# A retention layer's output projection as seven products over sums of halves, with the heads in a new order and the gated outputs through DRAM

## The chip, the cores and the metric

The kernel runs on one core of one Trainium2 chip. The metric is device time in microseconds (us) of the whole kernel. Five engines work beside each other, each through a list of instructions of its own: PE (matrix products; PEld is its weight load), DVE (vector), ACT (scalar functions and copies), POOL (the third elementwise engine) and SP, which here only issues DMAs. An engine runs its list in order and halts at an instruction whose inputs or buffers are not ready.

## The reference

One sequence of 1024 positions, width 1024, passes a retention layer and then a stick-breaking attention layer. The change lies in the first layer and in what stands right behind it:

```python
u = rms_norm(h, ret_norm_pre[i])
q, k, v, g = jnp.split(u @ ret_w_in[i], [...], axis=-1)
q = rope(split_heads(q, 4), pos)
k = rope(split_heads(k, 4), pos) * 256 ** -0.5
o = retention_chunkwise(q, k, v)          # 4 heads, values 512 wide
o = (o - mu) * lax.rsqrt(var + EPS)       # per position and head
o = merge_heads(o) * jax.nn.silu(g)       # 1024 x 2048
y = o @ ret_w_out[i]                      # 2048 -> 1024
h = h + rms_norm(y, ret_norm_post[i])
kv = rms_norm(h, kv_norm) @ w_kv          # keys, values of the next layer
```

Retention is causal. In chunks of 128 positions, `o` is (q k^T * decay) v inside a chunk plus q times a state that is carried on.

## The kernel before, in words

**Arithmetic.** All is float32. For a product each operand is written as a rounded part (ACT copies it to fp32r) and the rest (DVE subtracts), which is `split`. `mm3` makes a product of three PE matmuls: high by high, high by low, low by high. Most are 128x512: 128 rows out, 512 columns.

**Tiling.** The sequence is taken in two halves of 512, t=0 and t=1. Activations lie transposed, 128 channels by 512 positions a tile. PSUM has eight banks of 512 floats in four tags with two buffers each: `pma`, `pmb` for projections, `pz`, `po` for the retention heads.

**Projections.** `Group` makes a projection of 1024 by 1024 with seven products in place of eight, over sums and differences of halves of the weights, of the input and of the output (numbered 1 to 7; each is 48 PE matmuls). Six groups (v0, g0, k, q, v1, g1) feed the retention layer, six more (K, Q, V0, G0, V1, G1) the attention layer.

**Retention heads.** `AHead(t, h)` is one head of one half. `scores()` makes q k^T, `mix()` the outputs `o` into the `po` banks (four tiles of 128 positions by 512), and for t=0 the state that t=1 of the same head needs, which goes to DRAM (`st`) and is read back. An output tile leaves its bank in one way: DVE takes its statistics (BATCH_NORM_STATS2, AGGREGATE), POOL makes the reciprocal root from them with three small operations, ACT writes the normed tile `sgn`. Only then is the `po` bank free. `gate()` multiplies with the gate, transposes on PE into `pz` and splits the result into `oT`.

**Output projection before.** `outproj` runs once for each (t, h): eight tiles of 128x512, 12 matmuls each, added into `y`, which lies in DRAM (`y_d`) and is read and written once a head. Its matmuls stand between the PE work of the next head: while U=(t, h) goes through `mix` and `gate` and the head behind it through `scores`, the projection of the head ahead of U fills PE. The order of heads is (0,0), (0,1), (0,2), (0,3), (1,0), ... The first head stands beside product 4 of group g1.

**Behind it.** `a_post(t)` norms `y` (sum of squares, a column of reciprocal roots on POOL, turned into a row of 512 by `diag` and a matmul), adds x and takes the sum of squares of the result; `c_stats(t)` and `c_prep` make from it the operands of the six attention groups. `a_post(0)` runs beside heads (1,1) and (1,2), half its sums on POOL; `a_post(1)` beside the products 2 of the second to sixth group.

**Order.** The program isn't issued as written. All operations are recorded (one helper, line 229, emits every one, so all lines read L229). `merge` puts the side work between the main matmuls, and `Plan` sets each engine's order by its own costs. What it decides is seen only in the lists of instructions.

Of the kernel before, what the change touches and what calls it, by code (L numbers as in the profile page):

```python
# [10 lines left out]
F32 = mybir.dt.float32  # L11
# [7 lines left out]
NH = 4  # L19
# [438 lines left out]
def trunk(ctx, tc, xT, wts, gains, trig, ident_in, cols, grow_in, out):  # L458
# [4 lines left out]
    BUFS = dict(b=28, f=25, big=2, whl=3, small=24, col=8, ma=2, mb=2, z=2, o=2)  # L463
    GROUP = dict(xh="b", v="b", A="b", AT="b", S="b", ko="b", sgn="b", sc0="b", sc1="b", sc2="f", sc3="f", wraw="f", f2="f",
                 sg="f", vo="f", tab="f", acc="f", qk="big", oT="big")
# [245 lines left out]
    def sumsq(acc, src, c, eng):  # L711
        if c == 0:
# [63 lines left out]
    h_d = [[DRAM(f"h{t}{c}", F32) for c in range(4)] for t in range(2)]  # L776
    av_d = [[[rec.tile(dr, [128, 512], F32, f"av{t}{h}{b}", dram=True) for b in range(4)] for h in range(NH)] for t in range(2)]
# [10 lines left out]
    def a_prep():  # L788
# [122 lines left out]
    class AHead:  # L911
        def __init__(self, t, h):
            self.t, self.h, self.base = t, h, 48 + 4 * h

        def fetch(self):
            x, h = [], self.h
            for n in range(4):
                raw = S("f2", [512])
                dma(raw[:], aqk_d[self.t][h][n][:])
                x.append(hl("ko"))  # L920
                split((x[n][:, 0, :], x[n][:, 1, :]), raw[:], None if h < 2 else -1.0)
            self.q, self.k = x[:2], x[2:]
            self.v = []
# [8 lines left out]
        def out(self, y_d, acc=None, hold=None):  # L932
            return outproj(self.base, lambda: self.oT, y_d, self.h == 0, acc, None, hold)
# [33 lines left out]
        def mix(self):  # L967
# [69 lines left out]
            os = [lambda ib=ib: o(ib) for ib in range(4)] + [normed]  # L1037
# [4 lines left out]
            return [state_in] + os  # L1042

        def gate(self):
            o = S("qk" if self.h == NH - 1 else "oT", [4, 2, 512], F32R)
            self.oT = [o[:, e] for e in range(4)]

            def step(ib):
                on = self.on[ib]
# [9 lines left out]
    def a_post(t, y_d, acc, hold=None):  # L1059
# [13 lines left out]
        def load(k):  # L1073
            y, raw = box[k] = (hold[k % 4][:, k // 4], S("tab", [512])) if t else (S("vo", [512]), S("vo", [512]))
            if not t:
                dma(y[:], y_d[k])
            dma(raw[:], xT[128 * k:128 * k + 128, HT * t:HT * t + HT])

        def add(k):
            c2, c = divmod(k, 2)  # L1080
            y, raw = box[k]
            V.scalar_tensor_tensor(y[:], y[:], gcol(G_POST, k), box["rows"][:], ALU.mult, ALU.mult)
            (V if t else G).tensor_tensor(y[:], y[:], raw[:], ALU.add)
            dma(h_d[t][c2][:, 512 * c:512 * c + 512], y[:])

        def square(k):
            y, raw = box[k]
            if k == 0:
                A_.activation(box["acc"][:], y[:], AF.Square)
            else:  # L1090
                A_.activation(raw[:], y[:], AF.Square)
                (V if t else G).tensor_tensor(box["acc"][:], box["acc"][:], raw[:], ALU.add)
# [4 lines left out]
        return [stat1, stat2, row] + in_turn(8, 3 if t else 0, load, add, square) + [stat3]  # L1097
# [34 lines left out]
    def h_rows(t, i, hold=None):  # L1132

        raw = S("S", [2, 512]) if hold is None else hold[i]
        for c in range(0 if hold else 2):
            dma(raw[:, c], h_d[t][i // 2 + 2 * c][:, 512 * (i % 2):512 * (i % 2) + 512])
        V.tensor_tensor(raw[:], raw[:], rowh[t][:].unsqueeze(1).broadcast_to([128, 2, 512]), ALU.mult)
        return raw

    def c_prep(hold):  # L1140
# [16 lines left out]
        def early(i, c):  # L1157
            if c:
                X.raw[i] = h_rows(0, i)
# [27 lines left out]
    class Group:  # L1187
        def __init__(self, base, kind, gain, X, banks, order, early=(), keep=True):
# [8 lines left out]
            self.starts.update({n: banks4 for n in early})  # L1197
            self.onto = {n: m for n, m in ((6, 1), (7, 1), (4, 1), (3, 5)) if n not in early}
# [94 lines left out]
        def chunks(self, *which):  # L1293
# [27 lines left out]
            def done(n, b, p):  # L1321
# [9 lines left out]
                if n == 6 or n in (1, 2) and not k(3 - n) or n == 5 and 7 not in early:  # L1331
# [19 lines left out]
                elif n == 7:  # L1351
                    self.put(0, 1, b, plus(k(5), p), -1)
# [41 lines left out]
    class CPair:  # L1394
# [57 lines left out]
        def mix(self, hh):  # L1452
# [44 lines left out]
            def gate():  # L1497
                for e in range(2):
# [3 lines left out]
                    if j == 0:  # L1502
                        self.o = S("oT", [4, 2, 512], F32R)
                    x = self.oT[j] = self.o[:, j]
# [99 lines left out]
    def run():  # L1604
# [12 lines left out]
        def make_groups(base, kinds, X, early, keep):  # L1617
            order = [tuple(n for n in ((1, 2, 6, 5, 7, 3, 4) if at < 5 else (2, 1, 6, 5, 3, 7, 4)) if n not in early[at]) for at in range(6)]
            return order, [Group(base + 8 * at, kind, gain, X, sets[::-1] if at % 2 and at < 5 else sets, order[at], early[at], keep[at])
# [5 lines left out]
        order, groups = make_groups(0, kinds, X, early, (True, False, True, True, False, True))  # L1625
        H = [[AHead(t, h) for h in range(NH)] for t in range(2)]
# [29 lines left out]
        units = [(t, h) for t in range(2) for h in range(NH)]  # L1656
        post, acc = [], []
        for k, (t, h) in enumerate(units):
            U = H[t][h]
            if k == 0:  # L1660
                continue
            t0, h0 = units[k - 1]
            if t0 == 1 and h0 == 0:
                post = a_post(0, y_d[0], acc)
            if h0 == 0:
                acc = []
            side = [(post[:5], 0, 0)] if (t, h) == (1, 1) else [(post[5:] + c_stats(0), 0, 0)] if (t, h) == (1, 2) else []
            if (t, h) == (1, 3):
                hold = []
                Y, load, plain, late = c_prep(hold)  # L1670
                side = [(load, 0, 0)]
            nxt = H[units[k + 1][0]][units[k + 1][1]] if k + 1 < 8 else None
            def sides(U=U, side=side, nxt=nxt):
                x = [(U.mix() + U.give + U.gate(), 0, 0)]
                if nxt:
                    x.append((nxt.scores(), 0, 0))
                return x + side
            go(H[t0][h0].out(y_d[t0], acc if h0 == 3 else None), sides)
        X = Y
# [3 lines left out]
        go(groups[0].chunks(2))  # L1683
        go(H[1][3].out(y_d[1], acc, hold))
        post = a_post(1, y_d[1], acc, hold)
        ahead_of = [(at, 2) for at in range(1, 6) if early[at]]
        steps = [[(post[:3], 1, 0)], [(plain + post[3:6], 0, 0)], [(post[6:9], 0, 0)], [(post[9:], 0, 0)], [(c_stats(1) + late[:2], 0, 0)]]
        for k, (at, n) in enumerate(ahead_of):
            go(groups[at].chunks(n), lambda k=k: steps[k] if k < len(steps) else [])
# [117 lines left out]
```

## Time and profile before

| | us |
|---|---|
| time, median of 3 runs (lowest, highest) | 1635.08 (1632.72, 1636.35) |
| profiled execution, first to last instruction (its span) | 1629.8 |
| PE busy | 1619.7 |
| DVE busy | 1247.6 |
| ACT busy | 818.6 |
| POOL busy | 246.9 |

The profiled execution's own time is its span and a few us around it: the median stands 5.3 us above the span. In the trace the first head's `mix` lies at about 464 to 491 us, the out projections of heads at about 491 to 800, five products 2 of the attention groups at about 800 to 855. A matmul record's length is longer than the distance to the next one, since matmuls overlap; PE's rate is read from the starts of two neighbouring rows.

### The profile page before, as it was taken

How to read it: one execution, taken by the hardware profiler on the slowest of the kernel's cores; microseconds unless marked ns; L12 is line 12 of the kernel's file. 1: busy time of each engine (PE TensorE's matmuls, PEld its weight loads, DVE VectorE, ACT ScalarE, POOL GpSimd, SP SyncE). 2: the span in 40 equal slices, each digit the busy share in tenths (PEclk: the TensorE clock that was granted, in tenths of full speed). 3: DMA queues.
4: the chain of work that ended last, by engine and by line, in shares of the span. 5: the costliest groups of instructions: out<-in, count | busy, mean ns of one | idle time of the engine just before them, and what ended most of it. 6: DMA issues, size and time to landing. Idle time of an engine off the chain costs nothing.

```text
span 1629.8 us, 23078 instructions
## 1 busy us (share of the span) xinstructions
PE 1619.7 (99%) x7634; PEld 1346.5 (83%) x7634; DVE 1247.6 (77%) x1952; ACT 818.6 (50%) x1502; POOL 246.9 (15%) x328
## 2 busy tenths in 40 slices
PE   9999999999999999999999999999999999999998
PEld 7888888888888888888888888888888888888886
DVE  7998679795686777767569966758658886879897
ACT  7634332322576545533467544545445655536544
POOL 0000024230022114441000000000002222212420
PEclk9999999999999999999999999999999999999999
DMA  8774636486477788788486879639787869777884
GB/s 287 247 249 162 226 122 215 155 299 224 155 251 247 265 291 277 263 303 298 163 291 209 311 261 335 245 134 312 260 329 255 294 230 308 265 275 275 287 283 155
DMA packets 201400, 407.99 MB, mean 250 GB/s; under 512 B 22592, under 2 KB 23232, under 8 KB 201280
## 3 DMA queue, kind: packets, MB, share of 16 engines
q1 hardware_dynamic: 201280, 406.51, 72.4%
q8 instruction: 60, 0.98, 0.2%
q14 instruction: 60, 0.49, 0.1%
HBM read 286.89 MB, written 119.54 MB: 249 GB/s over the span
## 4 chain that ended last, share of the span: by engine, by line
PE 77%; DVE 2%; issue 0%; ACT 0%; DVEq 0%
PE pma L229 21%; PE pmb L229 21%; PE po L229 19%; PE pz L229 16%; DVE f L229 1%; DVE whl L229 0%; DVE wraw L229 0%; ACT f L229 0%; ACT small L229 0%; DVEq L1802 0%; DVE col L229 0%; DVE A L229 0%; DVEq L229 0%
## 5 line engine op out<-in xcount | busy, mean ns | idle before, releaser
L229 ACT ACTIVATE whl<-wraw 128x512 fp32r<-128x512 f32 (+1 forms) x392 | 231.9, 626 | 299.6 <-PE pmb L229 95.9
L229 DVE TENSOR_TENSOR whl<-wraw,whl 128x512 fp32r<-128x512 f32 x392 | 275.3, 725 | 129.6 <-ACT whl L229 129.1
L229 PE MATMUL pmb<-oT,whl 128*128 128x512 f32 x552 | 144.7, 395 | 0.0
L229 PE MATMUL pma<-oT,whl 128*128 128x512 f32 x552 | 141.9, 396 | 0.0
L229 PEld LDWEIGHTS pma<-oT,whl 128*128 128x128 f32 x552 | 101.4, 188 | 20.3 <-ACT oT L229 0.2
L229 PE MATMUL pma<-whl,xh 128*128 128x512 f32 x456 | 117.5, 392 | 0.1
L229 PEld LDWEIGHTS pmb<-oT,whl 128*128 128x128 f32 x552 | 100.8, 188 | 19.1
L229 PE MATMUL pmb<-whl,xh 128*128 128x512 f32 x456 | 116.1, 389 | 0.0
L229 POOL TENSOR_SCALAR_AFFINE_SELECT f<-f 128x128 f32<-128x128 f32 x64 | 34.3, 551 | 492.3 <-DMA wraw<-in_wts_dram 384.0
L229 PE MATMUL pma<-xh,whl 128*128 128x512 f32 x408 | 105.0, 392 | 0.0
L229 PE MATMUL pmb<-xh,whl 128*128 128x512 f32 x408 | 103.9, 390 | 0.0
L229 PE MATMUL pz<-ko,ko 128*128 128x512 f32 (+3 forms) x480 | 101.6, 332 | 0.0
L229 PEld LDWEIGHTS pmb<-whl,xh 128*128 128x128 f32 x456 | 85.6, 188 | 18.0
L229 PEld LDWEIGHTS pma<-whl,xh 128*128 128x128 f32 x456 | 84.9, 188 | 18.3 <-DVE whl L229 0.5
L229 POOL TENSOR_TENSOR f<-f,f 128x512 f32<-128x512 f32 x32 | 51.6, 1624 | 253.1 <-DVE f L229 225.4
L229 PEld LDWEIGHTS pmb<-xh,whl 128*128 128x128 f32 x408 | 76.4, 188 | 15.8
L229 PEld LDWEIGHTS pma<-xh,whl 128*128 128x128 f32 x408 | 75.9, 188 | 16.1 <-issue 0.5
L229 PEld LDWEIGHTS pz<-ko,ko 128*128 128x128 f32 x480 | 77.0, 189 | 10.5 <-ACT A L229 1.2
L229 PE MATMUL pma<-whl,oT 128*128 128x512 f32 x312 | 82.0, 398 | 0.5 <-ACT oT L229 0.3
L229 PE MATMUL pmb<-whl,oT 128*128 128x512 f32 x312 | 81.2, 392 | 0.0
L229 DVE SCALAR_TENSOR_TENSOR wraw<-wraw,gn,wraw 128x512 f32<-128x512 f32 x96 | 69.8, 745 | 14.2 <-ACT wraw L229 8.9
L229 PE MATMUL pz<-xh,whl 128*128 128x512 f32 x312 | 79.2, 389 | 0.0
(207 smaller groups left out, 3334.8 us busy)
## 6 DMA issues: line engine op xcount, KB each, us to landing
wraw<-in_wts_dram SPq DMA_DIRECT2D x559, 256.0 KB, 5.1
v<-v SPq DMA_DIRECT2D x64, 512.0 KB, 6.1
y<-f SPq DMA_DIRECT2D x112, 256.0 KB, 2.7
f<-y SPq DMA_DIRECT2D x88, 256.0 KB, 4.9
ko<-kq SPq DMA_DIRECT2D x40, 512.0 KB, 5.7
kq<-v SPq DMA_DIRECT2D x32, 512.0 KB, 6.4
s<-f SPq DMA_DIRECT2D x40, 256.0 KB, 2.9
f<-s SPq DMA_DIRECT2D x40, 256.0 KB, 4.6
```

The source lines that it names most:

```text
L229: f(*[_real(a) for a in o.args], **{k: _real(v) for k, v in o.kw.items()})
```

## The change

- The output projection is one `AOut`: for all of `y` seven products (1, 5, 3, 6, 7, 4, 2 in this order) over sums of the two sequence halves, of the two halves of the 2048 inputs (heads 0, 1 and heads 2, 3) and of the two halves of the outputs. A product is 4 units x 2 x 4 banks x 3 = 96 matmuls.
- Its operands are made on DVE and ACT in tiles of 128x1024 (`op` from the gated outputs, `whl` from the weights), each sum or difference first, then the split. The gated outputs go to DRAM (`o_d`, 16 stores of 512 KB) and come back as often as products need them (36 loads of 512 KB); the weights take 36 loads of 512 KB in place of 64 of 256 KB.
- The heads are in the order (0,0), (1,0), (0,1), (1,1), (0,2), (0,3), (1,2), (1,3), called U0 to U7 here. U0 to U3 stand beside products 7, 4, 5, 3 of g1, U4 to U7 beside products 1, 5, 3, 6 of `AOut`. Product 7 has no side work, product 4 has the first part of `a_post(0)`, product 2 the rest of it with `c_stats(0)` and the first operands of the attention groups.
- `y` stays in SBUF (`hold`), so `y_d` isn't written or read; `a_post(0)` makes all its sums on DVE. The six products 2 of the attention groups follow, with `a_post(1)` beside the first four and `c_stats(1)` beside the fifth.
- Buffers: the pools `big` (2) and `whl` (3) become one pool `w` (7), of which `op`, `on`, `oT`, `qk` and `whl` take their tiles.

By the two programs' lists, PE has 7510 instructions (before 7606), which is 96 matmuls of 128x512 fewer; DVE 1944 (1954), ACT 1484 (1496), POOL 311 (333), and SP issues 1302 DMAs (1398): 176 of 256 KB fewer, 88 of 512 KB more.

The diff, cut:

```diff
-    BUFS = dict(b=28, f=25, big=2, whl=3, small=24, col=8, ma=2, mb=2, z=2, o=2)
+    BUFS = dict(b=28, f=25, w=7, small=24, col=8, ma=2, mb=2, z=2, o=2)
...
+    o_d = [[[DRAM(f"o{t}{h}{n}", F32) for n in range(2)] for h in range(NH)] for t in range(2)]
...
         def gate(self):
...
-                split((o[:, :, 0, il], o[:, :, 1, il]), pt[:].rearrange("p (e n) -> p e n", e=4))
+                A_.activation(o[:, :, il], pt[:].rearrange("p (e n) -> p e n", e=4), AF.Copy)
+                if ib == 3:
+                    for n in range(2):
+                        dma(o_d[self.t][self.h][n][:], o[:, 2 * n:2 * n + 2].rearrange("p a b -> p (a b)"))
...
+    class AOut:
...
+            self.units = [(n, i) for n in (1, 5, 3, 6, 7, 4, 2) for i in range(4)]
+            self.get = ahead(28, lambda at: (self.weights(*self.units[at]), self.operand(*self.units[at])))
...
+        def operand(self, n, i):
...
+            x = S("op", [2, 1024], F32R)
+            if n in (1, 2, 3):
+                a = load(*{1: (1, 0), 2: (1, 1), 3: (0, 1)}[n])
+            elif n in (5, 7):
+                a, b = (load(1, 0), load(0, 0)) if n == 5 else (load(0, 1), load(0, 0))
+                V.tensor_tensor(a[:], a[:], b[:], ALU.subtract)
...
+            split(self.pieces(x), a[:])
+            return x
...
+        def chunk(self, n, i, kk):
...
+            for b in range(4):
+                cl = slice(512 * kk + 128 * b, 512 * kk + 128 * b + 128)
+                mm3(banks[b][:], w[:, 0, cl], w[:, 1, cl], x[:, 0, sl], x[:, 1, sl], n != 3 and i + kk == 0, i == 3 and kk == 1, goes_on=n == 3)
...
-            (V if t else G).tensor_tensor(y[:], y[:], raw[:], ALU.add)
+            V.tensor_tensor(y[:], y[:], raw[:], ALU.add)
...
-        return [stat1, stat2, row] + in_turn(8, 3 if t else 0, load, add, square) + [stat3]
+        return [stat1, stat2, row] + in_turn(8, 3, load, add, square) + [stat3]
...
+        order, groups = make_groups(0, kinds, X, early, (True, False, True, True, False, True), (1, 2, 6, 7, 4, 5, 3))
+        order[4] = (1, 6, 4, 5, 3)
+        U = [AHead(t, h) for t, h in ((0, 0), (1, 0), (0, 1), (1, 1), (0, 2), (0, 3), (1, 2), (1, 3))]
...
-                go(group.chunks(*order[at][:-2]))
-                go(group.chunks(7), lambda: [(H[0][0].scores(), 0, 0)])
-                go(group.chunks(4), lambda U=H[0][0]: [(U.mix() + U.give + U.gate(), 0, 0), (H[0][1].scores(), 0, 0)])
+                go(group.chunks(1, 2))
+                go(group.chunks(6), lambda: [(U[0].scores(), 0, 0)])
+                for k, n in enumerate((7, 4, 5, 3)):
+                    go(group.chunks(n), unit(k))
...
-            go(H[t0][h0].out(y_d[t0], acc if h0 == 3 else None), sides)
-        X = Y
+        hold, acc = [[None] * 4 for _ in range(2)], [[], []]
+        Y = AOut(48, hold, acc)
+        for k, n in enumerate((1, 5, 3, 6)):
+            go(Y.chunks(n), unit(4 + k))
+        go(Y.chunks(7))
+        X, load, plain, late = c_prep(hold)
+        post0, post1 = a_post(0, acc[0], hold[0]), []
+        go(Y.chunks(4), lambda: [(post0[:9], 0, 0)])
+        go(Y.chunks(2), lambda: [(post0[9:] + c_stats(0) + load, 0, 0)])
```

**SP, the states of the first head.** Before, the list has the two stores of the state of (0,0) with weight loads, sums of `y` and the next head's inputs between and behind them; the loads `ko<-st_73`, `ko<-st_74` of (1,0) stand some hundred rows further on. After, the same place reads (`av` and `ag` are a head's values and gates in DRAM, `on` the gated outputs, `o` their place in DRAM):

```order
L229 DMA st_73<-ko_4427 128x1024 [waits DMAHW3_49,DVE_49]
L229 DMA sg_4459<-ag_203 128x512 [waits DMAHW4_49]
L229 DMA st_74<-ko_4450 128x1024 [waits DMAHW5_49,DVE_49]
L229 DMA ko_4490<-st_73 128x1024 [waits DMAHW6_49,DMAHW3_49,PE_49]
L229 DMA sg_4513<-ag_204 128x512 [waits DMAHW7_49]
L229 DMA ko_4524<-st_74 128x1024 [waits DMAHW5_49,DMAHW0_49,PE_49]
L229 DMA o_105<-on_4480 128x1024 [waits DMAHW1_49,Activation_49]
L229 DMA o_106<-on_4480 128x1024 [waits DMAHW2_49]
```

The load of a state now stands three rows behind its store, and the loads and stores behind it on SP wait with it.

**PE, the outputs of a t=1 head.** Before, at head (0,1), whose outputs `po` have the out projection of (0,0) between them (`pma`, `pmb` from `oT`):

```order
L229 MATMUL pmb_5368<-oT_5175,whl_5145 128x512 x6
L229 MATMUL po_5381<-v_4567,sc_4857 128x512 x3
L229 MATMUL po_5381<-v_4569,sc_4964 128x512 x3
L229 MATMUL pmb_5368<-oT_5175,whl_5145 128x512 x6
L229 MATMUL pz_5406<-ko_4993,ko_5040 128x256 x3
L229 MATMUL pz_5406<-ko_5054,ko_5063 128x256 x3
L229 MATMUL pmb_5416<-oT_5175,whl_5145 128x512 x6
L229 MATMUL po_5430<-v_4567,sc_4857 128x512 x3
```

After, at U1=(1,0), beside product 4 of g1 (`pma`, `pmb` from `xh`); `ko_4490` and `ko_4524` are the states loaded above:

```order
L229 MATMUL po_4547<-v_4385,sc_4256 128x512 x3
L229 MATMUL po_4553<-ko_4524,ko_4043 128x512 x3
L229 MATMUL po_4553<-v_4385,sc_4256 128x512 x3
L229 MATMUL po_4553<-v_4394,sc_4341 128x512 x3
L229 MATMUL pmb_3825<-whl_4242,xh_1104 128x512
L229 MATMUL pmb_3831<-whl_4242,xh_1104 128x512 x3
L229 MATMUL po_4603<-ko_4490,ko_4034 128x512 x3
L229 MATMUL po_4603<-ko_4524,ko_4043 128x512 x3
L229 MATMUL po_4603<-v_4385,sc_4256 128x512 x3
L229 MATMUL po_4603<-v_4394,sc_4341 128x512 x3
L229 MATMUL po_4603<-v_4438,sc_4433 128x512 x3
L229 MATMUL po_4631<-ko_4490,ko_4034 128x512 x3
```

`po_4603` takes the bank of `po_4547`; between the end of the one and the start of the other stand 13 matmuls. U0 to U3 now have the 48 matmuls of a product of g1 beside them each, where a head had the 96 of an out projection; U4 to U7 have the 96 of a product of `AOut`.

**DVE, the norm behind the projection.** Before, at `a_post(0)`, the column of reciprocal roots (`small<-pz`, then POOL makes `col`) and its diagonal stand between other heads' work, with SBUF sums of `y` (`vo`) on DVE and POOL behind them:

```order
L229 TENSOR_SCALAR small_6659<-pz_6635 128x4 [waits PE_49]
L229 TENSOR_TENSOR sgn_6666<-sgn_6666,sg_6419 128x512 [waits DMAHW3_49,Activation_49]
L229 TENSOR_SCALAR sgn_6681<-ident,col_6664 128x128 [waits Pool_49]
L229 TENSOR_SCALAR sgn_6681<-ident,col_6664 128x128 x3
L229 SCALAR_TENSOR_TENSOR sgn_6681<-ident,col_6664,sgn_6681 128x128 [waits DVE_49] x4
L229 BN_STATS small_6701<-po_6672 128x6 [waits PE_49]
```

After, beside product 4 of `AOut`, whose operands `op` and `whl` are split between the steps:

```order
L229 TENSOR_SCALAR small_7355<-pz_7340 128x4 [waits PE_49,Pool_49]
L229 TENSOR_TENSOR whl_7299<-raw_7197,whl_7299 128x1024 [waits DMAHW0_49]
L229 TENSOR_TENSOR whl_7343<-raw_7223,whl_7343 128x1024 [waits DMAHW2_49,Activation_49]
L229 TENSOR_SCALAR sgn_7380<-ident,col_7359 128x128 [waits Pool_49]
L229 TENSOR_SCALAR sgn_7380<-ident,col_7359 128x128 x3
L229 SCALAR_TENSOR_TENSOR sgn_7380<-ident,col_7359,sgn_7380 128x128 [waits DVE_49] x4
L229 TENSOR_TENSOR op_7384<-raw_7211,op_7384 128x1024 [waits DMAHW1_49,Activation_49]
L229 TENSOR_TENSOR whl_7395<-raw_7291,whl_7395 128x1024 [waits DMAHW1_49,Activation_49]
L229 SCALAR_TENSOR_TENSOR S_7072<-S_7072,gn,acc_7409 128x512 [waits Activation_49]
```

Where a retention output stood between the steps of the norm, there are now the splits of the projection's last two products, and behind them eight products and sixteen sums of the norm on DVE alone.

More of the change, by code (lines that the diff above doesn't have):

```diff
@@ L1035, in normed, with first @@
                 self.on.append(on)
-            os = [lambda ib=ib: o(ib) for ib in range(4)] + [normed]
+            def first():
+                self.fetch_values()
+                o(0)
+            os = [first] + [lambda ib=ib: o(ib) for ib in range(1, 4)] + [normed]
             if self.t == 0:
@@ L1061, in a_post @@
+    def a_post(t, acc, hold):
         box = {}
@@ L1130, in c_stats, with h_rows @@
         return [dia, row]
[L1132 to L1136, printed above, removed]
+    def h_rows(t, i, hold):
+        raw = hold[t][i]
         V.tensor_tensor(raw[:], raw[:], rowh[t][:].unsqueeze(1).broadcast_to([128, 2, 512]), ALU.mult)
@@ L1187, in trunk, with __init__ @@
     class Group:
-        def __init__(self, base, kind, gain, X, banks, order, early=(), keep=True):
+        def __init__(self, base, kind, gain, X, banks, order, early=(), keep=True, alone=False):
             self.base, self.kind, self.gain, self.X = base, kind, gain, X
@@ L1330, in done @@
                     return
[L1331 removed]
+                if n == 6 or n in (1, 2) and not k(3 - n) or n == (7 if self.alone else 5) and 7 not in early:
                     kept[n, b] = copy(p)
@@ L1615, in run, with make_groups @@
         sets = (banks4, ("z", "z", "o", "o"))
-        def make_groups(base, kinds, X, early, keep):
-            order = [tuple(n for n in ((1, 2, 6, 5, 7, 3, 4) if at < 5 else (2, 1, 6, 5, 3, 7, 4)) if n not in early[at]) for at in range(6)]
-            return order, [Group(base + 8 * at, kind, gain, X, sets[::-1] if at % 2 and at < 5 else sets, order[at], early[at], keep[at])
+        def make_groups(base, kinds, X, early, keep, last=(2, 1, 6, 5, 3, 7, 4)):
+            order = [tuple(n for n in ((1, 2, 6, 5, 7, 3, 4) if at < 5 else last) if n not in early[at]) for at in range(6)]
+            return order, [Group(base + 8 * at, kind, gain, X, sets[::-1] if at % 2 and at < 5 else sets, order[at], early[at], keep[at], at == 5 and last[0] == 1)
                            for at, (kind, gain) in enumerate(kinds)]
@@ L1624, in run, with unit, sides @@
         early = ((2, 7), (2, 7), (), (), (2, 7), ())
-        order, groups = make_groups(0, kinds, X, early, (True, False, True, True, False, True))
-        H = [[AHead(t, h) for h in range(NH)] for t in range(2)]
+        order, groups = make_groups(0, kinds, X, early, (True, False, True, True, False, True), (1, 2, 6, 7, 4, 5, 3))
+        order[4] = (1, 6, 4, 5, 3)
+        U = [AHead(t, h) for t, h in ((0, 0), (1, 0), (0, 1), (1, 1), (0, 2), (0, 3), (1, 2), (1, 3))]
+        def unit(k):
+            def sides():
+                x = [(U[k].mix() + U[k].give + U[k].gate(), 0, 0)]
+                if k < 7:
+                    x.append((U[k + 1].scores(), 0, 0))
+                return x
+            return sides
         main = groups[0].chunks(2)
@@ L1682, in run @@
         order, groups = make_groups(64, kinds, X, early, (False,) * 6)
[L1683 to L1689, printed above, removed]
+        post = a_post(1, acc[1], hold[1])
+        steps = [[(post[:3], 2, 0)], [(plain + post[3:6], 0, 0)], [(post[6:9], 0, 0)], [(post[9:], 0, 0)], [(c_stats(1), 0, 0)], [(late[:2], 0, 0)]]
+        for at in range(6):
+            go(groups[at].chunks(2), lambda at=at: steps[at])
         P = [[CPair(t, p) for p in range(NPAIR)] for t in range(2)]
@@ L1774 @@
         units += [_in_units(wi[:, a:a + 512]), _in_units(wi[:, a + 512:a + 1024])]
-    for h in range(NH):
-        b = 512 * h
-        units.append(_out_units(wo[b:b + 512]))
+    for j in range(2):
+        for half in range(2):
+            units.append(_in_units(wo[1024 * half:1024 * half + 1024, 512 * j:512 * j + 512]))
     for w, a in ((wk, 0), (si, 0), (wk, 1024), (si, 1024), (wk, 2048), (si, 2048)):
```

160 lines of the change are left out of this document (111 added, 49 removed).

## The prediction

> **What bounds the kernel now.** I read the page's head and its busy times first, then the view of waits for PE, and last the windows of the part that changes.
>
> ```profile
> span 1629.8 us, 23078 instructions
> PE 1619.7 (99%) x7634; PEld 1346.5 (83%) x7634; DVE 1247.6 (77%) x1952; ACT 818.6 (50%) x1502; POOL 246.9 (15%) x328
> PEclk9999999999999999999999999999999999999999
> ```
> ```profile
> PE pz L229 <- DVE onesr L229: 1.4, 1, 1.4
> PE pma L229 <- ACT oT L229: 0.3, 1, 0.3
> PE pma L229 <- ACT whl L229: 0.2, 1, 0.2
> ```
>
> PE is busy for 99% of the span, its granted clock is full in all forty slices, and all that it ever waits for another engine is 1.9 us in three waits at the start (1.4 + 0.3 + 0.2). So the span is PE's own work: a matmul taken away is time taken away, and a wait that the change makes adds in full, since there is no slack on PE to take it up. No other engine's busy time matters until PE waits for it.
>
> ```profile
> 570.00:649.00 79.00, 79.00 (x378) 65.97 (x378) 59.93 (x104) 40.79 (x70) 22.85 (x37) 1.00 0.86 291
> 800.00:855.00 55.00, 55.00 (x248) 44.97 (x247) 34.63 (x57) 31.23 (x54) 2.46 (x2) 1.00 0.69 239
> 855.00:890.00 35.00, 35.00 (x156) 29.00 (x155) 35.00 (x55) 26.77 (x49) 0.00 (x0) 1.00 0.56 183
> ```
>
> The columns are the stretch, its length, the busy time of PE, PEld, DVE, ACT and POOL, then the granted clock, the DMA share and GB/s. In the head stage DVE has 60 of 79 us; in the last stretch it is busy for all 35 us and PE still loses nothing, because its work had been put early enough. A full DVE is thus no loss by itself; only a result that comes late is one.
>
> **What is removed.** The lists differ by 96 PE instructions, all 128x512 out-projection matmuls (768 before, 672 after); the heads, the groups and the transposes are the same in number.
>
> ```profile
> 583.66 2.88 PE L229 MATMUL pmb<-oT,whl 128*128 128x512 f32 x12
> 586.38 2.20 PE L229 MATMUL po<-v,sc 128*128 128x512 f32 x9
> ```
>
> Twelve of the removed kind start at 583.66 and the next group at 586.38, so one takes (586.38 - 583.66)/12 = 0.2267 us, and 96 take **21.8 us**. That is the gain, if nothing new waits. DMA bytes cancel (176 x 256 KB fewer, 88 x 512 KB more, both 44 MB). POOL's 22 sums go to nobody's cost or to DVE, which is counted below. The new split and sum operations of 128x1024 on DVE and ACT lie beside the PE products 1, 5, 3 and 6, some 153 us of PE by the list against some 121 us of DVE at the durations below; there I cost them at nothing. Without that cover they would cost up to 1.13 us apiece.
>
> **What is added: the state's round trip.** U1=(1,0) now follows U0=(0,0) at once, and its first outputs read the state that U0 has just stored.
>
> ```profile
> L229 SPq DMA_DIRECT2D st<-ko x8: 319/390/1062, 485.5 to 616.6; - x8
> L229 SPq DMA_DIRECT2D ko<-st x8: 378/426/677, 587.2 to 703.4; - x8
> DMA to landing us min/median/max: 2.7/5.8/7.4
> ```
> ```profile
> st<-ko SPq DMA_DIRECT2D x8, 512.0 KB, 5.0
> ko<-st SPq DMA_DIRECT2D x8, 512.0 KB, 6.1
> ```
> ```profile
> L229 DVE TENSOR_TENSOR f<-po,f 128x512 f32<-128x512 f32 x40 | 26.9, 685 | 1.4 <-PE po L229 1.4
> L229 ACT ACTIVATE ko<-f 128x512 fp32r<-128x512 f32 x48 | 29.3, 628 | 12.3 <-DMA f<-aqk 11.4 <-DVE f L229 0.6
> L229 DVE SCALAR_TENSOR_TENSOR ko<-f,ko 128x512 fp32r<-128x512 f32 x24 | 16.3, 698 | 1.1 <-ACT ko L229 1.0
> ```
>
> Before, the first store was at 485.5 and the first load at 587.2, a hundred us apart; the trip was free. Now between the last state matmul of U0 and the first that reads it PE's list holds 29 matmuls of 128x512 and 38 smaller ones, 10.7 us. The chain takes 0.69 (sum) + 0.63 (high part) + 0.70 (low part) = 2.0 us, then store and load: at their medians 5.0 + 6.1 = 11.1 us, at the shortest landing 2.7 + 2.7 = 5.4, at the longest 7.4 + 7.4 = 14.8. So U1 comes late by 2.4 us at the medians, by nothing at the shortest, by 6.1 at the longest. U2 to U3 has 12.5 us of PE and one DVE operation of 0.7 more ahead of the low part: late by 1.3, 0 or 5.0. Both together: 0, 3.7 or 11.1 us. The medians are from a stage that moved up to 291 GB/s (the row of 570 to 649 us), the shortest landings show what a free queue gives, and the place of the new trip lies between; I take **2 us**, the middle of the fast and the median case. Behind the waiting load stand on SP the stores of the gated outputs and the inputs of U2; U2's scores come some 20 us of PE later, which covers it. Behind PE's waiting matmul stands everything.
>
> **Added: less cover for the `po` banks.** U0 to U3 have 48 matmuls of a projection each where a head had 96. A bank is taken again after its tile's statistics (DVE), three small operations (POOL) and the normed copy (ACT).
>
> ```profile
> 697.31 0.70 DVE L229 BATCH_NORM_STATS2 small<-po 128x6 f32<-128x512 f32 x1 [0.48 <-PE po L229]
> 714.45 0.69 DVE L229 BATCH_NORM_STATS2 small<-po 128x6 f32<-128x512 f32 x1
> ```
> ```profile
> 699.27 1.28 POOL L229 TENSOR_TENSOR vo<-vo,vo 128x512 f32<-128x512 f32 x1
> 700.51 1.00 POOL L229 TENSOR_TENSOR small<-small,mhalf 128x1 f32<-128x1 f32 x1
> ```
> ```profile
> 702.95 0.78 ACT L229 ACTIVATE sgn<-po,small,small 128x512 f32<-128x512 f32 x1 [1.74 <-POOL small L229]
> 716.56 0.78 ACT L229 ACTIVATE sgn<-po,small,small 128x512 f32<-128x512 f32 x1 [0.69 <-POOL small L229]
> ```
>
> One turn of a bank took 703.73 - 697.31 = 6.4 us where POOL had sums of the norm (`vo`) in its list between the small operations, and 717.34 - 714.45 = 2.9 us where nothing was between. The change takes these sums off POOL. In the new list the nearest reuses in this stage are 13 matmuls, 13 x 0.2267 = 2.95 us, three times, then 3.2, 3.4, 3.7 and more. At 2.9 us a turn nothing waits; at 6.4 all do, and the differences over the stage add up to 40 us. The nearer row is the fast one, since POOL is empty; with some 0.3 us of other work between, three reuses wait 0.3 each: **1 us**.
>
> **Added: the norm of half 0 beside products 4 and 2.** From the last sum of product 7 to the first operand of the attention groups PE has 204 instructions, 46.1 us. DVE has in this stretch 26 of 128x512 with two inputs, 18 with a scalar as well, 13 of 128x1024, and 16 small ones for two diagonals.
>
> ```profile
> 827.48 0.74 DVE L229 SCALAR_TENSOR_TENSOR S<-S,gn,pz 128x512 f32<-128x512 f32 x1
> 828.13 0.68 DVE L229 TENSOR_TENSOR acc<-acc,tab 128x512 f32<-128x512 f32 x1
> ...
> 829.34 0.68 DVE L229 TENSOR_TENSOR acc<-acc,tab 128x512 f32<-128x512 f32 x1
> 829.94 1.40 DVE L229 SCALAR_TENSOR_TENSOR whl<-wraw,gn,whl 128x512 fp32r<-128x512 f32 x2
> ```
> ```profile
> 857.50 1.21 DVE L229 TENSOR_TENSOR S<-S,pz 128x1024 f32<-128x1024 f32 x1
> 858.63 0.68 DVE L229 SCALAR_TENSOR_TENSOR f<-S,S 128x512 f32<-128x512 f32 x1
> ```
> ```profile
> 660.45 1.01 DVE L229 TENSOR_SCALAR sgn<-ident,col 128x128 fp32r<-128x128 f32 x4
> 661.39 1.12 DVE L229 SCALAR_TENSOR_TENSOR sgn<-ident,col,sgn 128x128 fp32r<-128x128 f32 x4
> 662.49 0.70 DVE L229 BATCH_NORM_STATS2 small<-po 128x6 f32<-128x512 f32 x1
> ```
>
> From start to start: 0.60 (829.34 to 829.94), 0.65 (827.48 to 828.13), 1.13 (857.50 to 858.63), and 2.04 for a diagonal's eight. 26 x 0.60 + 18 x 0.65 + 13 x 1.13 + 2 x 2.04 = 15.6 + 11.7 + 14.7 + 4.1 = 46.1 us: as much as PE has. The first operand is needed some 2 us after PE's 46.1, so DVE may halt for 2 us. It has four places to halt, twice at the column (POOL) and twice at the row (PE, ACT):
>
> ```profile
> 805.82 0.75 DVE L229 SCALAR_TENSOR_TENSOR whl<-wraw,gn,whl 128x512 fp32r<-128x512 f32 x1 [3.42 <-ACT whl L229]
> ...
> 812.26 0.75 DVE L229 SCALAR_TENSOR_TENSOR S<-S,gn,pz 128x512 f32<-128x512 f32 x1 [3.58 <-PE pz L229]
> ```
>
> In the norm of half 1 DVE stood for 3.4 us ahead of the column and 3.6 ahead of the row, without loss to PE. In the new list two splits of 1.13 us stand at each of these places. Covered so, a halt costs 3.5 - 2.3 = 1.2 us at most, four 4.8, less 2 of slack: 2.8; with no halt 0; bare, 4 x 3.5 - 2 = 12. I take **1 us**, since the loop is short where POOL is empty.
>
> **Sum.** Span 1629.8 - 21.8 + 2 + 1 + 1 = 1612.0; the 5.3 us between span and median stay as they are, so **1617.3 us**, 1.1% faster.
>
> **The rivals.**
> *The state's trip decides* (0.15). Stores wait behind other traffic and take the long landings: 11.1 in place of 2 us gives 1626.4. For it: the halt is at a place without any other order, and landings reached 7.4. Against it: the shortest were 2.7. A halt would show as PE waiting for `ko<-st`. PE's clock bears on it:
>
> ```profile
> 1.38 3.53 PE L229 MATMUL pz<-onesr 128*128 128x512 f32 x8 [1.38 <-DVE onesr L229]
> 5.20 1.39 PE L229 MATMUL pma<-whl,oT 128*128 128x512 f32 x4 [0.30 <-ACT oT L229]
> ```
>
> After the idle start a matmul took 3.53/8 = 0.44 us, double the later 0.2267, until about 5 us. If a halt of over 3 us made PE as slow again for as long, some 15 matmuls would lose 0.21 us each, 3.2 us a halt. The Trainium skill, "TensorE: Matmul & The Clock Gate", Part 1, says that the clock falls to half after an idle window of about 3.4 us and comes back after as long a busy one. The start agrees; no wait behind the start is long enough to show it.
>
> *DVE decides behind the projection* (0.12): its halts are bare, 12 us in place of 1, 1628.3. For it: 46.1 against 46.1. Against it: the list has splits at each place.
>
> *Slower* (0.04): the `po` banks turn in 6.4 us though POOL is empty, since DVE and ACT have the operands' splits between the steps. The stage then waits 40 us, 1617.3 - 1 + 40 = 1656. It is slower than before from about 19 us of waits there, which is a turn of some 5 us.
>
> *DMA decides* (0.04). Product 7 has sixteen loads of 512 KB, 8.4 MB for its 96 x 0.2267 = 21.8 us, 385 GB/s, if none is early.
>
> ```profile
> GB/s 287 247 249 162 226 122 215 155 299 224 155 251 247 265 291 277 263 303 298 163 291 209 311 261 335 245 134 312 260 329 255 294 230 308 265 275 275 287 283 155
> ```
>
> The largest slice moved 335 GB/s; at that the loads take 25 us, 3.3 late: 1620.6. Against it: buffers let loads go one product ahead, and product 6 has only four of its own. The Trainium skill, "DMA: Bandwidth & Descriptors", Specifications, gives about 358 GB/s of HBM a core; by it the loads would take an estimated 23 us, 1.6 late. The trace stays below that figure in every slice.
>
> *It does nothing* (0.03): waits of all four kinds eat the 21.8 us, 1632 to 1638.
>
> **How the numbers follow.** The forecast has 0.62. The range goes from 1612.8 (no wait at all: 1635.1 - 21.8 = 1613.3, and half a us for the start) to 1627 (the trip at its longest, or DVE's halts nearly bare). Less than 0.2% (3.3 us) can't be told from no change: faster than 1631.8 has 0.92 (the forecast, the trip, most of DVE and DMA), within it 0.04, slower 0.04.
>
> **What would show it.** PE with 96 fewer matmuls at 0.2267 us and a full clock; few us of PE waiting, on `po` from the loaded `ko` at U1 and U3, on `sgn<-po` in U0 to U3, on `xh` behind product 2. I'd be wrong if PE waits for `op` or `whl` (DMA or DVE late in products 1 to 6), if waits at the banks come to over 5 us, or if the matmul's pitch changes.

## The result and the profile after

| | before | after |
|---|---|---|
| time, median of 4 runs (lowest, highest), us | 1634.40 (1632.72, 1636.35) | 1615.87 (1614.99, 1616.67) |
| ratio, 95% interval | | 0.9885 (0.9871 to 0.9899) |
| profiled span, us | 1629.8 | 1613.2 |
| PE busy, us | 1619.7 | 1600.7 |

The kernel is 1.15% faster; 1617.3 us was forecast, in a range of 1612.8 to 1627.0. The profiled execution itself took 1614.99 us, so that only 1.8 us lie around its span.

The page's head and busy times, then the view of PE's waits, of the changed kernel (columns of the latter: total us, times, longest):

```profile
span 1613.2 us, 22605 instructions
PE 1600.7 (99%) x7538; PEld 1327.9 (82%) x7538; DVE 1275.5 (79%) x1942; ACT 829.1 (51%) x1490; POOL 238.4 (15%) x306
PEclk9999999999999999999999999999999999999999
```
```profile
PE pz L229 <- DVE onesr L229: 1.4, 1, 1.4
PE po L229 <- ACT sgn L229: 1.1, 3, 0.4
PE pma L229 <- ACT whl L229: 1.0, 2, 0.5
PE pz L229 <- DVE acc L229: 0.3, 1, 0.3
PE pma L229 <- ACT xh L229: 0.2, 1, 0.2
```

PE is still the bound, at full clock. It now waits 4.0 us, 1.9 before. Three of these waits are at the `po` banks (1.1 us), one is for an operand of the attention groups (`xh`, 0.2), one for the sum of squares in the norm of half 1 (`acc`, 0.3). One of the two for `whl` (0.4 us, near 358 us, ahead of the heads) has no counterpart in the kernel before. None is for the state, for `op` or for the weights of the out projection.

The windows, by stage: heads beside g1, heads beside the products of `AOut`, product 7, products 4 and 2, and what follows (columns as in the prediction):

```profile
430.00:543.00 113.00, 112.58 (x565) 93.67 (x565) 81.73 (x158) 69.42 (x125) 33.77 (x64) 1.00 0.70 245
543.00:700.00 157.00, 156.21 (x757) 129.83 (x756) 125.95 (x180) 87.19 (x133) 46.36 (x61) 1.00 0.79 295
700.00:722.00 22.00, 22.00 (x102) 18.29 (x101) 21.94 (x25) 12.27 (x15) 0.00 (x0) 1.00 0.77 284
722.00:769.00 47.00, 47.00 (x216) 38.94 (x216) 44.84 (x73) 28.16 (x41) 3.85 (x2) 1.00 0.57 198
769.00:800.00 31.00, 30.51 (x135) 24.04 (x134) 30.70 (x50) 20.69 (x37) 1.44 (x1) 1.00 0.63 213
```

DVE is full from 700 us on: 44.8 of 47 us beside products 4 and 2, where 46.1 were worked out. PE loses nothing there, and half a us behind it.

The views leave a part of each halt out. A matmul's record is 0.39 us long and the next one starts after 0.227, so the first 0.16 us of a halt count as busy. Adding up each matmul's distance to the next start, less 0.2267 us (128x512; for the smaller forms less their median in the traces, 0.11 to 0.18 us), gives, stage by stage, in us:

```
stage                        before   after   after, 2nd and 3rd profile
up to 270 us                    3.1     3.4     4.4   4.1
from there to the heads         0.4     0.8     1.3   1.0
heads and out projection        1.9     4.5     4.4   4.3
first products 2, norm 1        1.0     2.3     2.3   2.4
the rest, to the end            6.0     6.4     6.5   6.3
```

So the change loses 2.4 to 2.6 us in the heads' stage and 1.3 us behind it. Another 0.4 to 0.9 us is lost ahead of the heads, mostly at the wait for `whl` near 358 us, which all three profiles have. The pool that `whl` takes its tiles from is new there, and the products of the last groups stand in another order; which of the two makes the wait isn't shown. The first row differs by 1.0 us between profiles of the same kernel.

### The profile page after: what moved, and what is told of

Read it like the earlier page. It is cut to its first block, busy times and chain, and to the rows that moved or that the text cites. A ratio compares the mean times of both kernels' runs of the same rounds, so it can differ in the third digit from the quotient of the medians.

```text
span 1613.2 us, 22605 instructions
## 1 busy us (share of the span) xinstructions
PE 1600.7 (99%) x7538; PEld 1327.9 (82%) x7538; DVE 1275.5 (79%) x1942; ACT 829.1 (51%) x1490; POOL 238.4 (15%) x306
## 2 busy tenths in 40 slices
DMA packets 187573, 405.85 MB, mean 252 GB/s; under 512 B 21057, under 2 KB 21697, under 8 KB 187457
## 4 chain that ended last, share of the span: by engine, by line
PE 74%; DVE 2%; issue 1%; POOL 1%; ACT 1%; DMA 0%; DVEq 0%; SPq 0%; POOLq 0%; ACTq 0%
PE pma L229 21%; PE pmb L229 20%; PE po L229 18%; PE pz L229 15%; DVE f L229 1%; DMA wraw<-in_wts_dram 0%; DVE S L229 0%; POOL f L229 0%; POOL small L229 0%; DVE acc L229 0%; ACT f L229 0%; DVE small L229 0%; ACT sgn L229 0%; DVE wraw L229 0%; ACT whl L229 0%
## 5 line engine op out<-in xcount | busy, mean ns | idle before, releaser
L229 ACT ACTIVATE whl<-wraw 128x512 fp32r<-128x512 f32 (+1 forms) x328 | 194.3, 626 | 240.3 <-PE po L229 73.0
L229 DVE TENSOR_TENSOR whl<-wraw,whl 128x512 fp32r<-128x512 f32 x328 | 228.5, 722 | 108.8 <-ACT whl L229 108.0
L229 PE MATMUL pma<-whl,xh 128*128 128x512 f32 x480 | 125.3, 393 | 0.4 <-ACT whl L229 0.4
L229 PE MATMUL pmb<-whl,xh 128*128 128x512 f32 x480 | 122.7, 389 | 0.0
L229 PEld LDWEIGHTS pmb<-whl,xh 128*128 128x128 f32 x480 | 90.0, 188 | 18.9
L229 POOL TENSOR_TENSOR f<-f,f 128x512 f32<-128x512 f32 x32 | 56.0, 1759 | 248.5 <-DVE f L229 222.5
L229 DVE SCALAR_TENSOR_TENSOR wraw<-wraw,gn,wraw 128x512 f32<-128x512 f32 x96 | 70.4, 748 | 24.9 <-ACT wraw L229 18.8
L229 PE MATMUL pma<-op,whl 128*128 128x512 f32 x336 | 89.5, 396 | 0.0
L229 PE MATMUL pmb<-op,whl 128*128 128x512 f32 x336 | 86.1, 390 | 0.0
L229 ACT ACTIVATE AT<-pz 128x512 fp32r<-128x512 f32 (+1 forms) x96 | 45.9, 491 | 65.0 <-PE pz L229 64.8
L229 PE MATMUL po<-xh,whl 128*128 128x512 f32 x312 | 79.2, 389 | 0.0
```

The costliest lines, as they stand in the source:

```text
L229: f(*[_real(a) for a in o.args], **{k: _real(v) for k, v in o.kw.items()})
```

## The experiments

Times are medians; the changed kernel took 1615.87, 1615.68 and 1615.80 us in three comparisons, and each kernel is set against the one beside it on its chip, or, where none was beside it (the heads apart for the first time, the second kernel with slow turns, the two on the norm), against 1615.68. Where a kernel adds instructions at their place of issue, all others stay in the order of the changed kernel.

### What 96 matmuls are worth

The kernel before, with one of the three products left out in one or two of the four input tiles:

```diff
-                mm3(p[:], w[:, 0, n], w[:, 1, n], oT()[e][:, 0, :], oT()[e][:, 1, :], e == 0, e == 3)
+                if e == 1 or e == 2 and c % 2:
+                    MM(p[:], w[:, 0, n], oT()[e][:, 0, :], start=False, stop=False)
+                    MM(p[:], w[:, 1, n], oT()[e][:, 0, :], start=False, stop=False)
+                else:
+                    mm3(...)
```

> The kernel before, with 96 of its 768 out-projection matmuls left out (the high-by-low product of one or two of four input tiles in each output tile); everything else stays. Theory (PE's work is the time, 0.2267 us a matmul): 21.8 us faster than before, 1612 to 1613 us; the changed kernel then pays some 3 us for what it adds. Rival (the removed matmuls covered something, or cost what they take with their switches, 0.233 us): no gain beyond 15 us, or 22.4 us.

It took 1600.20 us, against 1632.73 for the kernel before beside it: ratio 0.9804 (0.9789 to 0.9818), 32.5 us less. The expectation had the count wrong: the edited function also serves the attention layer's output for one half of the sequence. The two groups of its matmuls, before and then here, tell how many went:

```profile
L229 PE MATMUL pmb<-oT,whl 128*128 128x512 f32 x552 | 144.7, 395 | 0.0
L229 PE MATMUL pma<-oT,whl 128*128 128x512 f32 x552 | 141.9, 396 | 0.0
```
```profile
L229 PE MATMUL pmb<-oT,whl 128*128 128x512 f32 x492 | 131.7, 396 | 0.0
L229 PE MATMUL pma<-oT,whl 128*128 128x512 f32 x492 | 126.9, 396 | 0.0
```

The page of this run has 7490 matmuls where before had 7634, 144 fewer: 120 in these two groups and 24 of the last head's, whose operand is named `qk`. 32.5/144 = 0.226 us each, the 0.2267 of the prediction. Nothing was hidden behind the removed matmuls: 96 are worth 21.7 us, whatever else the change does.

### The same kernel again

> The changed kernel once more, beside the others on the same chip. If the 18.5 us between the medians are the change's and the 16.6 us between the two profiled spans a matter of single executions, the time is 1614 to 1617 us and the span some 1.8 us less. Waits of PE some 4 us again, at the same places (po banks in the heads with op and whl beside them, first operands behind product 2).

1615.68 us, ratio 0.9896 (0.9882 to 0.9911), span 1614.7. The waits at the banks are again 1.1 us. What varies lies ahead of the heads: the waits for `whl` and for the first norm, 1.5 us between the two profiles.

### The state's trip

Two kernels: the state made late by two copies, and the heads put apart.

```diff
+   # ahead of the load of the state, h < 2
+   sx_d[h][e] <- st_d[h][e], then st_d[h][e] <- sx_d[h][e]     (e = 0, 1)
```

> The changed kernel, every engine's order kept, with the state of heads (0,0) and (0,1) copied from DRAM to DRAM and back ahead of its load, so that it lands some two copies later, 6 to 10 us. In the profiled run of the changed kernel the states had landed 0.45 us (U1) and 2.2 us (U3) ahead of the matmul that reads them. Theory (the trip is just hidden, and what it is late is paid in full): U1 late by 5.5 to 9.5 us, U3 by 4 to 8, so 9 to 17 us slower than the changed kernel, PE waiting for the state's DMA at both places. Rival (PE has other slack there): under 3 us slower. If PE's clock falls in a wait of over 3 us, some 3 us more at each place, seen as matmuls at 0.44 us behind the wait.

1634.52 us, 18.8 us slower than the changed kernel, as slow as the kernel before. PE's waits in this run, and its timeline at U1:

```profile
PE po L231 <- DMA ko<-st: 12.9, 2, 6.6
```
```profile
470.45 2.93 PE L231 MATMUL po<-ko,ko 128*128 128x512 f32 x6 [6.62 <-DMA ko<-st]
473.17 1.75 PE L231 MATMUL pma<-whl,xh 128*128 128x512 f32 x4
474.76 0.62 PE L231 MATMUL pmb<-whl,xh 128*128 128x512 f32 x2
475.22 0.84 PE L231 MATMUL po<-ko,ko 128*128 128x512 f32 x3
```

The first number is the start: PE halts for 6.6 us, and then six matmuls take 473.17 - 470.45 = 2.72 us, 0.45 each, four more 0.40 each; from 474.76 they are at 0.23 again. That is 2.0 us on top of the halt; behind the second one, at U3, the starts give 1.7. The two halts with 12.9 us and these 3.7 make 16.6 of the 18.8. The granted clock of the stretch 460 to 480 us shows it:

```profile
460.00:480.00 20.00, 13.33 (x56) 10.61 (x55) 4.18 (x10) 3.18 (x7) 1.79 (x6) 0.83 0.72 252
```

The Trainium skill, "TensorE: Matmul & The Clock Gate", Part 1, puts the fall of the clock at an idle window of about 3.4 us and its return at as long a busy one. By it an estimated eight matmuls of 0.45 us fit into that stretch and lose some 1.8 us, which agrees with the 2.0 and 1.7 us here; no run here measures how long a halt has to be. The prediction's 3.2 us came from some 15 matmuls, more than fit into such a stretch at 0.44 us each. In the runs below halts of up to 2.0 us left the clock at full in one kernel, and in another it fell behind one of 1.4 us.

```diff
-        U = [... ((0, 0), (1, 0), (0, 1), (1, 1), (0, 2), (0, 3), (1, 2), (1, 3))]
+        U = [... ((0, 0), (0, 1), (1, 0), (1, 1), (0, 2), (0, 3), (1, 2), (1, 3))]
```

> The changed kernel with heads in the order (0,0), (0,1), (1,0), (1,1), (0,2), ...: a head's state now has a whole other head between its store and its load. Theory (in the changed kernel the trip was hidden, by 0.45 and 2.2 us): the same time within 1.5 us, 1614 to 1617. Rival (my forecast's term of 2 us for the trip is real, hidden in other waits): 2 us faster, under 1614.

1614.08 us, ratio 0.9882 (0.9867 to 0.9896): between the two expectations. So it was run again beside the changed kernel, on one chip.

> The order of heads with the states apart once more, on one chip with the changed kernel. If its 1.6 us were noise, within 0.8 us of the changed kernel; if the bank turns in U0 to U3 are better placed so (0.3 us of waits in place of 1.1 in its profile), 1 to 2 us faster.

> The changed kernel once more, for the comparison with the one ahead: 1614 to 1617 us.

1613.53 us (1613.04 to 1614.45) beside 1615.80 us (1615.62 to 1617.07): no run of the one reaches the other, 2.3 us. Ratios to before are 0.9875 (0.9860 to 0.9890) and 0.9890 (0.9875 to 0.9905), whose intervals overlap, since they carry the spread of the kernel before. It is not the trip: in the changed kernel PE waits for no state. The second kernel's waits in the changed part are

```profile
PE pmb L229 <- DVE S L229: 0.3, 1, 0.3
PE po L229 <- ACT sgn L229: 0.3, 1, 0.3
PE pz L229 <- DVE sc L229: 0.2, 1, 0.2
```

0.3 us at the banks where the changed kernel beside it has 0.8 (1.1 in the two other profiles), and its sum of the heads' stage, as in the table, is 3.3 us against 4.3. That accounts for 1.0 of the 2.3 us. The waits that are gone are not in U0 to U3, as was expected, but at U4 and U5, whose heads and side products are the same in both kernels. The turns of U4 to U7 take 4.5 us on average here and 5.3 in the changed kernel. The order is planned anew for this kernel, so other work has moved too, and the rest isn't settled.

### The banks' turn

> The changed kernel, every engine's order kept, with one more POOL operation (a power of 128x8, some 2 to 2.8 us by the 0.87 us of 128x1 and 1.7 us of 128x4) in each of the sixteen bank turns of U0 to U3. The turn there was 3.9 us on average; it becomes some 6.2. Theory (13 to 20 matmuls of cover between reuses, so every turn beyond 3 to 4 us is paid): 20 to 40 us slower than the changed kernel, PE waiting for the normed copy at nearly every bank of U0 to U3. Rival (the banks have cover to spare): under 5 us slower.

1614.61 us, no slower. The kernel didn't do what was meant: the added operation stood ahead of one that waits for DVE, and ran while POOL had nothing to do. The turns of U0 to U3 were 3.8 us as without it. So it was put behind that wait:

```diff
                 G.tensor_tensor(r[:], mv[:, 1:2], cc[:, 16 + 4 * h + ib:17 + 4 * h + ib], ALU.add)
+                # U0 to U3
+                G.tensor_tensor(slow[:], ones[:, 0:8], mhalf[:, 0:8], ALU.pow)
                 G.tensor_tensor(r[:], r[:], mhalf[:, 0:1], ALU.pow)
```

> The changed kernel, orders kept, with the power of 128x8 (1.75 us in the last run, where it ran in POOL's idle time ahead of the turn and lengthened nothing) now between the two small operations of each of the sixteen turns of U0 to U3, so that each turn is 1.75 us longer, 5.6 in place of 3.9 us on average. Theory (13 to 20 matmuls, 3 to 4.5 us, between reuses): the eight to twelve nearest reuses wait 1 to 2.5 us each, 12 to 22 us slower than the changed kernel. Rival (there is other slack in the banks): under 5 us slower.

1628.29 us, 12.6 us slower. Its groups, waits and two of the places:

```profile
L1026 POOL TENSOR_TENSOR slow<-ones,mhalf 128x8 f32<-128x8 f32 x16 | 28.3, 1766 | 0.0
```
```profile
PE po L229 <- ACT sgn L229: 9.9, 8, 2.0
```
```profile
454.47 0.98 PE L229 MATMUL po<-v,vo 128*128 128x512 f32 x3 [1.99 <-ACT sgn L229]
...
473.66 1.65 PE L229 MATMUL po<-ko,ko 128*128 128x512 f32 x6 [1.53 <-ACT sgn L229]
```

The turns of U0 to U3 went from 3.87 to 5.23 us on average (statistics' start to normed copy's end, sixteen each), 1.36 us more, and six waits for the normed copy stand there where one did (the two others of the eight are those of U4 and U5). The banks have next to no cover: 9.9 us of wait, and some 0.16 more at each that the records hide, make most of the 12.6. The granted clock stayed full, 1.00 in 430 to 560 us. By this slope (12.6 us for 1.36), as an estimate, turns in U0 to U3 some 2 us longer than the change has, near 6 us, would make the kernel as slow as before; the prediction said some 5. By the same slope turns of 6.4 us would cost some 23 us, where the prediction has 40.

### The norm of half 0 on DVE

```diff
+   # ahead of the column of reciprocal roots of half 0, on DVE, 20 times
+   slow[:] = onesr[:] + ident[:]                                  (128x128)
```

> The changed kernel, orders kept, with twenty more DVE operations of 128x128 (some 4 us) ahead of the column of the norm of half 0, in the stretch where DVE has 44.8 of 47 us. Theory (DVE and PE have the same work there, so no slack is left): 3 to 4 us slower than the changed kernel, the wait at the first operands behind product 2. Rival (PE isn't bound by DVE there, the two halts of 0.8 and 1.0 us and the operands made early take it up): under 1 us slower.

1623.95 us, 8.3 us slower. The twenty took more than expected, and the halt came elsewhere: DVE's and PE's timelines of this run,

```profile
733.13 6.47 DVE L1192 TENSOR_TENSOR slow<-onesr,ident 128x128 f32<-128x128 f32 x20
739.51 0.15 DVE L231 TENSOR_SCALAR small<-pz 128x4 f32<-128x4 f32 x1
```
```profile
742.87 0.77 PE L231 MATMUL pz<-sgn,onesr 128*128 128x512 f32 x1 [4.95 <-DVE sgn L231]
743.43 1.06 PE L231 MATMUL pma<-op,whl 128*128 128x512 f32 x2
```

739.51 - 733.13 = 6.4 us of DVE cost PE 5.0 us at the matmul that turns the column into a row, and then a slow clock: 0.91 of full in 740 to 760, another 1.7 us by the starts. The two make 6.7 of the 8.3. DVE had 1.4 us to spare at this place. PE doesn't wait for the first operands, as was expected, but 25 us earlier: the row's matmul stands in PE's list at a fixed place, and product 4 behind it waits with it.

```diff
-            V.tensor_tensor(y[:], y[:], raw[:], ALU.add)
+            (V if t else G).tensor_tensor(y[:], y[:], raw[:], ALU.add)
```

> The changed kernel with the eight additions of x in the norm of half 0 on POOL again, as before (the sums of squares stay on DVE). DVE has 8 x 0.60 = 4.8 us less in a stretch in which it stood still for under 2 us of 47. Theory (DVE full there, PE behind it by some 1 us at the first operands): 0.5 to 1.5 us faster, the waits for operands behind product 2 gone. Rival (POOL takes 1.3 to 1.8 us an addition and DVE waits for it in the chain of the norm): 1 to 5 us slower.

1618.11 us, ratio 0.9907 (0.9892 to 0.9922), 2.4 us slower. The interval overlaps with that of the changed kernel (0.9882 to 0.9911), and the four runs go from 1615.59 to 1620.52, so the times alone say no more than that it isn't faster. The trace shows the rival: DVE's timeline of this run, where POOL adds beside it (an addition there takes 1.71 us on average):

```profile
749.62 1.78 DVE L229 SCALAR_TENSOR_TENSOR S<-S,gn,acc 128x512 f32<-128x512 f32 x1
751.32 0.68 DVE L229 TENSOR_TENSOR acc<-acc,tab 128x512 f32<-128x512 f32 x1
751.92 1.78 DVE L229 SCALAR_TENSOR_TENSOR S<-S,gn,acc 128x512 f32<-128x512 f32 x1
```

The product with the row takes 1.78 us there where it takes 0.74 without POOL beside it. Each of the two starts within an addition on POOL (749.17 to 750.85, 751.48 to 753.15) and ends 0.55 us behind that addition's end. Of the 4.8 us that DVE was to save, products like these give most back; and PE waits for an operand of product 2 (`op`) and for the first ones of the attention groups (`xh`):

```profile
PE pma L229 <- DVE xh L229: 1.7, 2, 1.0
PE pma L229 <- DVE op L229: 1.4, 1, 1.4
```

The clock fell behind the wait for `op`, though that was only 1.4 us long:

```profile
760.30 0.74 PE L229 MATMUL pma<-op,whl 128*128 128x512 f32 x2 [1.43 <-DVE op L229]
...
762.26 1.05 PE L229 MATMUL pma<-op,whl 128*128 128x512 f32 x2
763.12 1.05 PE L229 MATMUL pmb<-op,whl 128*128 128x512 f32 x2
```
```profile
762.00:766.00 4.00, 4.00 (x12) 3.17 (x12) 3.75 (x8) 0.00 (x0) 1.93 (x1) 0.57 0.99 347
```

From 762.26 on matmuls take 0.43 us each, and by the starts the slow ones cost 1.6 us, as much as the wait. Why the clock fell here, and not behind the 2.0 us of the slow turn, isn't shown. So the sums on DVE, full as it is, are no worse a place here.

### The DMAs of product 7

```diff
+   # ahead of each of the sixteen loads of product 7
+   xx_d[k] <- o_d[0][0][i % 2]                        (512 KB, DRAM to DRAM)
```

> The changed kernel, orders kept, with sixteen more DMAs of 512 KB from DRAM to DRAM, one ahead of each load of product 7's operands and weights. In the changed kernel these loads are issued from 670 to 690 and from 705 us, land after 5 to 11 us at up to 356 GB/s, and PE waits for none. Theory (DMA is near its limit there, but the loads are early by a few us): 16.8 MB more read and written at some 350 GB/s put the loads off by some 20 to 45 us, of which the lead takes 5 to 10: PE waits for op or whl, 10 to 35 us slower. Rival (loads lie far ahead of their use): under 3 us slower.

1622.89 us, 7.1 us slower, less than expected. PE's timeline at the start of product 7 and the window ahead of it:

```profile
702.19 1.03 PE L231 MATMUL pz<-ident,sgn 128*128 128x128 f32 x8
707.59 2.78 PE L231 MATMUL pma<-op,whl 128*128 128x512 f32 x6 [4.36 <-DVE f L231]
710.17 2.02 PE L231 MATMUL pmb<-op,whl 128*128 128x512 f32 x6
```
```profile
680.00:700.00 20.00, 20.00 (x94) 16.57 (x93) 10.81 (x15) 7.09 (x9) 4.23 (x8) 1.00 1.01 421
```

DVE is busy for only 10.8 of 20 us there and stands for loads, which put its emptying of the banks off, and PE halts once, for 4.4 us, again with six matmuls at 0.43 us behind it. The expectation overrated the load: the profile counts a copied byte once (414.23 MB in all against 405.85), so that the copies are 8.4 MB more and not 16.8 in its GB/s, and the DMAs moved 421 GB/s and not 350. Without the copies the loads are in time, so the prediction's rival that DMA decides stood off by no more than these 8.4 MB.

## Why the prediction was right, point by point

**What bounds it, and what is removed.** Right. PE's time is the kernel's, and 0.2267 us a matmul was measured again as 0.226 with everything else left alone.

**The state's trip, 2 us.** Mis-sized; it cost nothing. At U1 the last of the chain is, by the landings of the first store and load and by PE's timeline,

```profile
st<-ko SPq DMA_DIRECT2D x2, 512.0 KB, 3.5
```
```profile
ko<-st SPq DMA_DIRECT2D x1, 512.0 KB, 5.3
```
```profile
461.16 0.70 PE L229 MATMUL pma<-whl,xh 128*128 128x512 f32 x2
461.69 1.55 PE L229 MATMUL po<-ko,ko 128*128 128x512 f32 x6
```

3.5 is the median of the two stores. The first one was issued at 452.52; its load was issued at 455.97 and landed 5.27 us later, at 461.24; PE came at 461.69. So the trip took 8.7 us, against the 11.1 of the medians and the 8.7 that the list had left for it (10.7 - 2.0). The chain was as tight as the prediction had it. The 2 us were a middle between the lateness of two cases, 0 and 3.7 us; at a trip half way between their lengths (8.2 us) nothing is late. The long trip showed what it would have cost.

**The banks, 1 us.** Right in size by the view, 1.1 us (1.6 by the starts), and wrong in place. The reuses of 13 matmuls at U1 didn't wait; one wait is at U0, two are at U4 and U5, beside the products of `AOut`. At U4:

```profile
567.35 1.67 PE L229 MATMUL po<-ko,ko 128*128 128x512 f32 x6 [0.43 <-ACT sgn L229]
```
```profile
562.51 0.69 DVE L229 BATCH_NORM_STATS2 small<-po 128x6 f32<-128x512 f32 x1
```
```profile
563.60 0.86 POOL L229 TENSOR_SCALAR_AFFINE_SELECT sc<-sc 128x256 fp32r<-128x256 f32 x1 [9.42 <-DVE sc L229]
564.43 1.15 POOL L229 TENSOR_TENSOR small<-small,cc 128x1 f32<-128x1 f32 x1
565.66 0.55 POOL L229 TENSOR_TENSOR small<-small,mhalf 128x1 f32<-128x1 f32 x1
```
```profile
566.51 0.78 ACT L229 ACTIVATE sgn<-po,small,small 128x512 f32<-128x512 f32 x1 [3.96 <-POOL small L229]
```

This turn is 567.29 - 562.51 = 4.8 us. Those of U4 to U7 were 5.3 us on average, those of the second four heads before 4.4 and those of U0 to U3 3.9. The prediction took the splits beside products 1, 5, 3 and 6 at nothing, since DVE has time enough there (126 of 157 us). In the turn shown POOL has a select of scores ahead of its small operations; at U5 a split of 1.21 us stands on DVE between the statistics and their sum. So splits can lengthen a turn, but with the heads apart the same splits leave the turns of U4 to U7 at 4.5 us: it depends on where the order puts them. The 96 matmuls of those products cover the turns but for 0.8 us.

**The norm of half 0, 1 us.** Right in size: 0.5 us of waits, 1.3 by the starts, 0.3 of the waits in the norm of half 1 behind it. The sum of DVE's work, 46.1 us for 46.1, was the measure. The slack of 2 us at the first operands isn't what bounds it: when DVE was made late, PE halted first at the matmul of the row, where 1.4 us were to spare.

**The sum.** By the medians the change gained 18.5, 17.1 and 18.8 us in three comparisons, so of the 21.7 us that 96 matmuls are worth it gives 2.9 to 4.7 back; 4 were forecast. That this fits is in part luck. The 2 us of the trip weren't paid; in their place stand some 1.5 us more than forecast in the heads' stage, in short gaps of which no view lists all, and 0.4 to 0.9 us ahead of the heads, at which the prediction had nothing. The span says less: 1612.0 us was forecast, and three profiles have 1613.2, 1614.7 and 1614.0. Every time on record with its own span stands 1.7 to 2.2 us above it. So the 5.3 us were no distance around a span; the profiled execution of before, whose own time isn't on record, was some 3.5 us quicker than the median. Adding the 5.3 us back did no harm, since it made the sum one of medians: 1635.1 - 21.8 + 4.

**The rivals.** None came true. Four were brought about. Late states cost 18.8 us, turns 1.36 us longer 12.6, 6.4 us more of DVE 8.3 and 8.4 MB more of copies 7.1. So the forecast was right by narrow cover, and not by wide.

## What to carry to other kernels

Where one engine is busy for 99% and never waits, a saved instruction is worth its start-to-start distance in full, and the rest of the question is how late each new wait comes; find for each new chain the distance that the order leaves it, and set it against the chain's length. A DRAM round trip that fits by half a us costs nothing, and one that is late costs all of its delay and a slow clock behind it. Another order of independent work is worth a try even so: the heads apart made this kernel 2.3 us faster (1613.53 us), though not by the trip. Take the distance between a span and a time from one and the same execution.

## What the runs showed of the hardware

- Halts of PE of 4.4 to 6.6 us cost another 1.6 to 2.0 us each, eight or nine matmuls at about 0.43 us (granted clock 0.83 and 0.91 in stretches of 20 us). The halts of up to 2.0 us with the slow turn cost only themselves (clock 1.00), but one of 1.4 us with the sums on POOL was followed by a clock of 0.57 over 4 us.
- DMA moved 421 GB/s over 20 us. The Trainium skill, "DMA: Bandwidth & Descriptors", Specifications, gives about 358 GB/s for a core's share of HBM; the window, with DRAM copies in it, passes that by the profile's count of bytes moved, which has a copied byte once.
- Twenty DVE additions of 128x128 take 0.32 us each back to back, 6.4 us in all, for a quarter of the elements of an operation of 0.60 us.
